# Second gate product by seven products, with its weight sums made in the up stages and half of the late embedding after the last MLP

## The chip, the cores and the metric

The kernel runs on one core of a Trainium2 chip. The metric is the device time of one execution in microseconds (us), and the number to predict is the median over several runs. A core has five engines that each execute their own queue of instructions in order: PE (matrix products), DVE (elementwise vector work), ACT (scalar functions and casts), POOL, and SP, which here issues the DMAs. They meet at semaphores.

## The reference

Two layers on `x` of 1024 tokens by 1024 features in fp32. Layer 0 mixes tokens by a convolution module, layer 1 by sliding-window attention; both then have an MLP of 4096 hidden features and a gated embedding. The part around the change is the end of each layer:

```python
x = layer_norm(DEEPNORM_ALPHA * x + y, mix_ln_g[i], mix_ln_b[i])
x = layer_norm(DEEPNORM_ALPHA * x + sq_relu_mlp(x, mlp_w_up[i], mlp_w_down[i]),
               mlp_ln_g[i], mlp_ln_b[i])
x = x + (p[i] @ ple_w_proj[i]) * jax.nn.sigmoid(x @ ple_w_gate[i])
```

`p[i] @ ple_w_proj[i]` (1024x256 by 256x1024) is called the embedding below, `x @ ple_w_gate[i]` (1024x1024 by 1024x1024) the gate.

## The kernel before

**Precision.** An fp32 operand is split into two fp32r parts: ACT casts the hi part, DVE subtracts it to get the lo part (`split`). Each product is three matmuls, hi·hi, hi·lo and lo·hi (`mm3`, 565), each 128x512 as a rule. So each product of 128 rows, 128 inner and 512 columns costs PE three matmuls, and each operand costs an ACT cast and a DVE subtraction before PE can use it.

**Buffers.** Each tag of `SLOTS` (line 54) is a small set of buffers in SBUF; `wh` and `wl` hold five weight units (128x1024 hi and lo), `ps` and `tr` the PSUM banks, `zz` and `v` one buffer each. `self.x[t]` holds token tile t as two 128x512 halves; `xTh`/`xTl` hold the transposed tokens, hi and lo. `Stream` (484) loads weight units in order as slots come free and splits them: `add` appends, `get` takes, `done` frees, `pump` loads.

**Stages.** `program` (line 1840 on) runs `conv`, `mlp(0)`, `ple(0)`, `attention`, `mlp(1)`, `ple(1)`. `attention` ends with `embed(1, (0, 1), "t")` (1713): 16 groups of 6 matmuls that compute the embedding of layer 1, copied to SBUF and stored to DRAM (`proj`), to be read back by `ple`. `mlp` (1225) works by seven products instead of eight (Strassen-Winograd) in its up half, a loop over pairs of hidden blocks numbered `m`, and in its down half (`down_seven`, 1367), whose last call adds up `x`, lets DVE and POOL do the layer norm of tiles 0 to 7 and transposes each tile by PE into PSUM, from where `to_xT` (603) splits it into `xTh`/`xTl`. Two pairs of each up half (`SUMS`) also make sums of down weights (`down_sums`, 1110). `ple` (1442) is the plain gate product: two column halves of four weight units, per token tile 24 matmuls per half, then sigmoid on ACT, multiply and add on DVE, and the store to `out`. Token tile 7's second half is done in two 256-column pieces (`last_tile`), so that little remains after the last matmul.

**Order.** A list scheduler (`Recorder.schedule`, 341) simulates the engines with a table of costs and fixes the queue of every engine. Instructions are taken by when their inputs are ready, then by a priority, the order of the program plus the shift of a `later(...)` block. All instructions are emitted by one line, L480, hence that line in every row of the profile. Nothing is reordered at run time: an instruction that waits holds all behind it on its engine.

Of the kernel before, what the change touches and what calls it, by code (L numbers as in the profile page):

```python
# [21 lines left out]
HT = 512  # L22
# [38 lines left out]
             ps=6, tr=2, sc=0, pv=0)  # L61


LATE = 100
EMBED_BY = 150
HELD, HELD_BY = 6, 200
HEAD = (4, 2)
# [20 lines left out]
SLACK = 900.0  # L88
LOADED = 1500.0
# [393 lines left out]
class Stream:  # L483


    def __init__(self, em):
        self.em = em
        self.units = []
        self.tiles = []
        self.head = 0  # L490
        self.freed = 0

# [20 lines left out]
class Emit:  # L513
    def __init__(self, tc, d):
        self.tc = tc
        self.nc = Recorder()
        self.d = d
        self.hid_tags = ("A", "X")


    def const(self, name, shape, dt):
# [78 lines left out]
    def blocks(self, a):  # L600
        return [a[:, j * P : (j + 1) * P] for j in range(4)]

    def to_xT(self, xt, t):

        for q in range(2):
            pv = self.transpose4(self.blocks(xt[q]), SLACK).rearrange("p (a b) -> p a b", a=4)
            sl = (slice(None), slice(4 * q, 4 * q + 4), slice(t * P, (t + 1) * P))
            self.split(pv, self.xTh[sl], self.xTl[sl])

    def phases_to_xT(self, h):  # L610

# [20 lines left out]
    def layer_norm(self, t, gb, spill=None):  # L632

        nc = self.nc
        xt = self.x[t]
        mean, scale = self.stats(xt)
        for q in range(2):
            nc.vector.scalar_tensor_tensor(out=xt[q], in0=xt[q], scalar=mean, in1=gb[0][q], op0=ALU.subtract, op1=ALU.mult)
        for q in range(2):
            nc.vector.scalar_tensor_tensor(out=xt[q], in0=xt[q], scalar=scale, in1=gb[1][q], op0=ALU.mult, op1=ALU.add)  # L640
        self.to_xT(xt, t)
# [467 lines left out]
    def down_sums(self, i, k):  # L1109
# [12 lines left out]
            nc.sync.dma_start(self.wsum[i][n][:, cols], out)  # L1122
        nc.slack = 0.0

    def first_operands(self, i):
# [111 lines left out]
    def mlp(self, i):  # L1237
        nc, d, ws = self.nc, self.d, self.ws
        tags, xtags = (dict(zip((2, 1, 3, 4), "XAEB")), "EB") if i == 0 else (dict(zip((2, 1, 3, 4), "XEAB")), "AB")
        first, pairs = list(range(HEAD[i])), list(range(HEAD[i], NFF, 2))  # L1240
        ws.add(*[d["w_up"][i, f] for f in first])
        for f in pairs:
            ws.add(*self.pair_units([d["w_up"][i, f + k] for k in range(2)]))

        us = ws.get(len(first))
        for h in range(2):
            for f in first:
                self.store(i, f, (f % 2, h), self.up(f, h, us[f]))
# [100 lines left out]
    def down_seven(self, i, cs, ready, end):  # L1349

        nc, d = self.nc, self.d
        sub = ALU.subtract
        n = len(cs)

        def A(tag, what):
            return [self.quarter(tag, self.hid[i][c, what]) for c in cs]
# [47 lines left out]
        if ready:  # L1404
            one = product(ready, [(0, 0)])
# [6 lines left out]
            two = product(spot(A("wh", "s3"), S(3), 1, 0), [(1, 1)])  # L1412
# [4 lines left out]
        a11, b11 = A("wh", (0, 0)), B("wl", 0, 0)  # L1417
# [11 lines left out]
        product(formed(s2, t2), [(1, 0)], one)  # L1429
        product(formed(A("wh", "s1"), t1), [(1, 1)], one)  # L1430
        s4 = A("wh", "s4")
        if end:
            gb = self.load_row("g", d["mlp_g"][i : i + 1]), self.load_row("g", d["mlp_b"][i : i + 1])
        product(formed(s4, b22), [(0, 1)], one, last=end)
# [5 lines left out]
    def ple(self, i):  # L1440
        nc, d, ws = self.nc, self.d, self.ws
        for cc in range(2):
            ws.add(*[d["w_gate"][i, cc, u] for u in range(4)])
        for cc in range(2):
            us = ws.get(4)
            cs = slice(cc * HT, (cc + 1) * HT)
            for g in GATE_GROUPS[i][cc]:
                if i == 1 and cc == 1 and NT - 1 in g:
                    self.last_tile(us, cs)
                    break  # L1450
                pss = self.tok_group(g, us)
                for ps, t in zip(pss, g):
                    xt = self.x[t][cc]
                    pr = self.sb("t")
                    nc.sync.dma_start(pr, self.proj[i][t][:, cs])
                    s = self.sb("t")
                    nc.scalar.activation(s, ps, AF.Sigmoid)
                    nc.vector.tensor_tensor(out=s, in0=s, in1=pr, op=ALU.mult)
                    nc.vector.tensor_tensor(out=xt, in0=xt, in1=s, op=ALU.add)
                    if i == 1:  # L1460
                        nc.sync.dma_start(d["out"][t * P : (t + 1) * P, cs], xt)
                    else:
                        h, f = t // PH, t % PH
# [3 lines left out]
            ws.done(4)  # L1467

    def last_tile(self, us, cs):

# [141 lines left out]
    def attention(self):  # L1612
# [189 lines left out]
    def program(self):  # L1802
# [36 lines left out]
        self.wsum = [{k: nc.tile(f"wsum{i}_{k}", (P, 1024), F32, "DRAM") for k in range(1, 5)} for i in range(2)]  # L1839
        self.ws = Stream(self)  # L1840
        self.setup()
        self.conv()
# [116 lines left out]
```

## Time and profile before

| | us |
|---|---|
| median of 3 runs | 2125.28 (2124.98 to 2126.82) |
| the profiled execution | 2127.52 |
| span of its instructions | 2125.8 |
| PE busy in the span | 2115.8 (100%) |
| PE weight loads busy | 1762.0 (83%) |
| DVE busy | 1560.1 (73%) |
| ACT busy | 1046.2 (49%) |
| POOL busy | 201.1 (9%) |

The span is from the first to the last instruction of the slowest (here the only) core; the profiled execution is longer by 1.7 us that lie around it. In rows of a timeline the first number is the start in us from the span's start, the second the duration, then engine, line, operation, `out<-in` with the names of buffers, and the shape; brackets hold idle time before the instruction and what ended it. In rows of windows each engine has its busy time in the window and, in brackets, how many instructions that is.

### The profile page before, as it was taken

The page shows a single profiled execution, that of the slowest core. Times are in us where ns is not written, and L with a number is a line of the kernel's source. Part 1 is how long each engine was busy: PE and PEld are TensorE (multiplying, and loading weights), DVE is VectorE, ACT ScalarE, POOL GpSimd, SP SyncE. Part 2 cuts the span into 40 slices and gives each one's busy share as a digit, 9 for nine tenths or more (in the row PEclk, how much of TensorE's full clock was granted, in tenths as well). Part 3 has the DMA queues.
Part 4 walks back from the last instruction along what each step waited for, and adds up shares of the span by engine and source line. Part 5 has one row for each costly group of instructions (what it writes and reads, how often), then busy time and mean ns, then how long its engine had stood idle before and what let it go on. Part 6 is the DMA issues. An engine that isn't in the chain of part 4 may idle for free.

```text
span 2125.8 us, 28547 instructions
## 1 busy us (share of the span) xinstructions
PE 2115.8 (100%) x10067; PEld 1762.0 (83%) x10067; DVE 1560.1 (73%) x2359; ACT 1046.2 (49%) x1888; POOL 201.1 (9%) x391
## 2 busy tenths in 40 slices
PE   9999999999999999999999999999999999999999
PEld 7888888888888888888889888888888888888887
DVE  8766868966566787889554798796755658878993
ACT  7555743555555433341333797365555563333321
POOL 0000141000000200000000566100000011000010
PEclk9999999999999999999999999999999999999999
DMA  7679882347457955540567672364654598445223
GB/s 249 195 204 278 279 216 99 105 163 258 168 179 277 257 184 172 179 129 25 167 194 224 213 239 63 111 197 146 223 187 136 182 339 238 149 160 189 88 70 104
DMA packets 208078, 384.61 MB, mean 181 GB/s; under 512 B 28736, under 2 KB 82496, under 8 KB 207936
## 3 DMA queue, kind: packets, MB, share of 16 engines
q1 hardware_dynamic: 200880, 369.96, 53.0%
q0 software_dynamic: 6912, 12.59, 3.3%
q8 instruction: 79, 1.29, 0.2%
q14 instruction: 63, 0.52, 0.1%
q10 hardware_dynamic: 144, 0.26, 0.0%
HBM read 263.98 MB, written 114.56 MB: 178 GB/s over the span
## 4 chain that ended last, share of the span: by engine, by line
PE 95%; DVE 2%; DMA 2%; ACT 1%; issue 0%; POOL 0%; SPq 0%; DVEq 0%; ACTq 0%; POOLq 0%
PE ps L480 73%; PE tr L480 22%; DMA raw<-in_w_up_dram 1%; DVE A L480 1%; DVE wl L480 0%; DMA wh<-hid 0%; ACT z L480 0%; DVE sm L480 0%; DMA X<-in_xT_dram 0%; ACT t L480 0%; DVE t L480 0%; ACT wh L480 0%; DVE xTl L480 0%; POOL sm L480 0%; SPq L480 0%
## 5 line engine op out<-in xcount | busy, mean ns | idle before, releaser
L480 DVE TENSOR_TENSOR wl<-raw,wh 128x1024 fp32r<-128x1024 f32 (+2 forms) x144 | 151.6, 1053 | 141.4 <-ACT wh L480 141.1
L480 PE MATMUL ps<-xTl,xTh 128*128 128x512 f32 x628 | 244.3, 389 | 0.0
L480 PE MATMUL ps<-xTh,xTl 128*128 128x512 f32 x628 | 244.3, 389 | 0.0
L480 PE MATMUL ps<-xTh 128*128 128x512 f32 x628 | 244.1, 389 | 0.0
L480 PE MATMUL ps<-xTh,wh 128*128 128x512 f32 x608 | 238.7, 393 | 0.4 <-ACT xTh L480 0.3
L480 PE MATMUL ps<-xTl,wh 128*128 128x512 f32 x608 | 238.6, 392 | 0.1
L480 PE MATMUL ps<-xTh,wl 128*128 128x512 f32 x608 | 237.8, 391 | 0.0
L480 ACT CAST wh<-raw 128x1024 fp32r<-128x1024 f32 (+2 forms) x144 | 131.4, 913 | 200.8 <-PE ps L480 98.4
L480 PE MATMUL ps<-wl,xTh 128*128 128x512 f32 (+1 forms) x424 | 162.3, 383 | 0.0
L480 PE MATMUL ps<-wh,xTh 128*128 128x512 f32 (+1 forms) x424 | 161.5, 384 | 0.0
L480 PE MATMUL ps<-wh,xTl 128*128 128x512 f32 (+1 forms) x424 | 160.8, 380 | 0.4 <-DVE xTl L480 0.4
L480 DVE TENSOR_TENSOR wl<-g,wh 128x512 fp32r<-128x512 f32 x140 | 92.5, 686 | 90.0 <-ACT wh L480 90.0
L480 ACT CAST wh<-g 128x512 fp32r<-128x512 f32 x140 | 82.7, 621 | 150.1 <-PE ps L480 98.3
L480 ACT CAST xTh<-wh 128x1024 fp32r<-128x1024 f32 x78 | 81.9, 1050 | 123.2 <-PE ps L480 101.5
L480 PEld LDWEIGHTS ps<-xTl,xTh 128*128 128x128 f32 x628 | 117.9, 188 | 24.6
L480 PEld LDWEIGHTS ps<-xTh,xTl 128*128 128x128 f32 x628 | 117.9, 188 | 24.4
L480 PEld LDWEIGHTS ps<-xTh 128*128 128x128 f32 x628 | 117.9, 188 | 24.3
L480 PEld LDWEIGHTS ps<-xTh,wh 128*128 128x128 f32 x608 | 114.3, 188 | 25.8 <-ACT xTh L480 1.0
L480 PEld LDWEIGHTS ps<-xTh,wl 128*128 128x128 f32 x608 | 114.2, 188 | 23.4
L480 PEld LDWEIGHTS ps<-xTl,wh 128*128 128x128 f32 x608 | 114.3, 188 | 22.2 <-DVE xTl L480 0.8
L480 DVE TENSOR_TENSOR xTl<-wh,xTh 128x1024 fp32r<-128x1024 f32 x78 | 95.1, 1220 | 32.9 <-ACT xTh L480 32.8
L480 DVE TENSOR_TENSOR xTl<-wl,xTh 128x1024 fp32r<-128x1024 f32 x80 | 97.3, 1218 | 3.4 <-ACT xTh L480 3.4
(318 smaller groups left out, 4952.6 us busy)
## 6 DMA issues: line engine op xcount, KB each, us to landing
wh<-hid SPq DMA_DIRECT2D x80, 512.0 KB, 4.5
raw<-in_w_up_dram SPq DMA_DIRECT2D x64, 512.0 KB, 3.8
wl<-in_w_down_dram SPq DMA_DIRECT2D x60, 512.0 KB, 4.6
hid<-t SPq DMA_DIRECT2D x95, 256.0 KB, 2.4
hid<-zz SPq DMA_DIRECT2D x68, 256.0 KB, 3.5
raw<-hid SPq DMA_DIRECT2D x30, 512.0 KB, 4.3
z<-scr SPq DMA_DIRECT2D x32, 256.0 KB, 3.9
proj<-t SPq DMA_DIRECT2D x32, 256.0 KB, 3.8
```

The costliest lines, as they stand in the source:

```text
L480: getattr(getattr(nc, o.eng), o.name)(*a, **k)
```

## The change

- The gate of layer 1 (`ple_seven` in place of `ple(1)`) is done by seven products of quarters (512 tokens by 512 inner by 512 columns) in place of eight.
- Its sums of weights are made by `gate_sums` at four pairs in all of the two up loops (`GATE_SUMS`). Each call loads four 128x512 pieces of `w_gate`, makes four sums on DVE, splits them (ACT casts to the tag `zz`, DVE subtractions) and stores hi and lo to DRAM (`gpart`). `gate_made` later loads them straight into `wh` and `wl`, two 512 KB loads per unit in place of one load and a split.
- The forms of tokens that the seven products need are made after the last layer norm by `row_forms`. For tiles 0 to 3 ACT also copies each transposed half to a buffer `rows[t]`. For tiles 4 to 7 DVE does eight operations of 128x512 per tile (`s3`, `s2`, four lo parts, `s1`, `s4`) where it did two lo parts; four further lo parts follow in `ple_seven`.
- `attention` ends with the embedding of column half 0 alone (8 groups of 6 matmuls); half 1 is called between `mlp(1)` and `ple_seven`, where the two units of `pT` are loaded and split once more. `AHEAD` gives the stream's loads from there on an earlier priority.
- In the last products, partial sums that PE no longer keeps in PSUM are copied by ACT and added by DVE (`copy`, `plus`): 12 copies and additions. Tile 7 has two 256-column pieces again.

```diff
+AHEAD = 300
+GATE_SUMS = (7, 9), (1, 3)
+GATE_TAG = 'zz'
...
     def pump(self):
...
-            self.tiles.append(u() if callable(u) else self.em.prep(u))
+            with self.em.nc.later(-self.ahead):
+                self.tiles.append(u() if callable(u) else self.em.prep(u))
...
+    def turned_copy(self, to, t, q):
+        pv = self.transpose4(self.blocks(self.x[t][q]), SLACK)
+        self.nc.scalar.copy(to, pv)
+        return to
+
+    def row_forms(self, xt, t):
...
+        if t < 4:
...
+            for q in range(2):
+                self.turned_copy(self.rows[t][q], t, q)
+                hi, lo = self.spot(q, t)
+                v = self.rows[t][q].rearrange("p (a b) -> p a b", a=4)
+                self.split(v, hi, lo)
+            return
+        r = self.rows[t - 4]
+        p0, p1 = (self.transpose4(self.blocks(xt[q]), SLACK) for q in range(2))
...
+        s3 = self.sb("z")
+        tt(out=s3, in0=r[0], in1=p0, op=sub)
+        s2 = self.sb("z")
+        tt(out=s2, in0=p1, in1=s3, op=sub)
+        self.split(four(p1), *self.spot(1, t))
+        x2 = [self.sb("X", F32R) for k in range(2)]
+        self.split(s2, *x2)
+        tt(out=r[0], in0=s2, in1=r[0], op=add)
+        w = self.sb("E", F32R, 2 * HT)
+        x1 = w[:, 0:HT], w[:, HT : 2 * HT]
+        self.split(r[0], *x1)
+        tt(out=r[1], in0=r[1], in1=s2, op=sub)
+        self.split(four(s3), *self.spot(0, t))
...
+    def gate_sums(self, k):
...
+        for j, q, tag in ((0, 0, "v"), (0, 1, "A"), (1, 1, "z"), (1, 0, "z")):
+            b[j, q] = self.sb(tag)
+            cols = slice(k % 2 * HT, (k % 2 + 1) * HT)
+            nc.sync.dma_start(b[j, q], self.d["w_gate"][1, q, 2 * j + k // 2][:, cols])
...
+        for n, out, x, y in ((1, b11, b12, b11), (3, b12, b22, b12), (2, b22, b22, b11), (4, b21, b21, b22)):
+            nc.vector.tensor_tensor(out=out, in0=x, in1=y, op=sub)
+            hs[n] = out
+        for n in (3, 1, 4, 2):
+            hi, lo = self.sb(GATE_TAG, F32R), hs[n].bitcast(F32R)
+            nc.scalar.copy(hi, hs[n])
+            nc.sync.dma_start(self.gpart[n, 0][:, cols], hi.bitcast(F32))
+            nc.vector.tensor_tensor(out=lo, in0=hs[n], in1=hi.bitcast(F32), op=sub)
+            nc.sync.dma_start(self.gpart[n, 1][:, cols], hs[n])
...
+            if m in GATE_SUMS[i]:
+                self.gate_sums(GATE_SUMS[i].index(m) + i * len(GATE_SUMS[0]))
...
+    def ple_seven(self, i):
...
+        order = [[w[0, 0], w[0, 1]], [w[0, 2], w[0, 3]]]
+        made = {n: [lambda n=n, u=u: self.gate_made(n, u) for u in range(2)] for n in range(1, 5)}
+        order += [made[2], made[1], [w[1, 2], w[1, 3]], made[3], made[4]]
...
+        us = ws.get(2)
+        two = [self.ps() for t in range(5)]
+        pieces = [(t, two[t], slice(0, HT)) for t in range(3)]
+        pieces += [(3, two[3 + k][:, 0:256], slice(k * 256, (k + 1) * 256)) for k in range(2)]
+        for t, ps, cols in pieces:
+            part(ps, F[3], us, t, False, cols)
+            finish(t + 4, 1, plus(c22[t][:, cols], ps), cols)
+        ws.done(2)
+        us = ws.get(2)
+        for t, ps, cols in pieces:
+            part(ps, plain[1, 1], us, t, True, cols)
+            finish(t + 4, 0, plus(c21[t][:, cols], ps), cols)
...
-        self.embed(1, (0, 1), "t")
+        self.embed(1, (0,), "t")
...
-        self.ple(1)
+        self.ws.ahead = AHEAD
+        self.embed(1, (1,), "t")
+        self.ple_seven(1)
```

How the queues change at three places:

**DVE in the last layer norms.** `B_...` are halves of a token tile, `sm` its statistics, `g` the gains, `xTl` the lo part of the transposed tokens. Before, where the lo parts of tile 4 stand between the layer norms of tiles 5 and 6:

```order
2287 L480 SCALAR_TENSOR_TENSOR B_2857_16007<-B_2857_16007,sm_3038_18032,g_3001_17652 128x512
2288 L480 SCALAR_TENSOR_TENSOR B_2858_16009<-B_2858_16009,sm_3038_18032,g_3002_17657 128x512
2289 L480 SCALAR_TENSOR_TENSOR B_2857_16007<-B_2857_16007,sm_3040_18050,g_3004_17673 128x512
2290 L480 TENSOR_TENSOR xTl_341<-ps_3056_18196,xTh_340 128x4x128
2291 L480 TENSOR_TENSOR xTl_341<-ps_3058_18234,xTh_340 128x4x128
2292 L480 SCALAR_TENSOR_TENSOR B_2858_16009<-B_2858_16009,sm_3040_18050,g_3005_17678 128x512
2293 L480 BN_STATS sm_3042_18064<-B_2861_16017 128x6
2294 L480 BN_STATS sm_3047_18104<-B_2863_16021 128x6
2295 L480 TENSOR_TENSOR xTl_341<-tr_3059_18238,xTh_340 128x4x128
2296 L480 BN_AGGR sm_3043_18069<-sm_3042_18064 128x2
```

Now the lines of tile 5, where `z` is `s3` and `s2`, `bo` the buffers of `rows[1]`, and `X` and `E` the lo parts of the forms that the products read:

```order
2336 L483 SCALAR_TENSOR_TENSOR B_2885_16067<-B_2885_16067,sm_3076_18143,g_3031_17709 128x512
2337 L483 TENSOR_TENSOR z_2895_16102<-bo_2838_15890,tr_3113_18336 128x512
2338 L483 SCALAR_TENSOR_TENSOR B_2887_16072<-B_2887_16072,sm_3076_18143,g_3032_17714 128x512
2339 L483 TENSOR_TENSOR z_2897_16122<-ps_3128_18410,z_2895_16102 128x512
2340 L483 TENSOR_TENSOR xTl_349<-z_2895_16102,xTh_348 128x4x128
2341 L483 TENSOR_TENSOR bo_2838_15890<-z_2897_16122,bo_2838_15890 128x512
2342 L483 TENSOR_TENSOR xTl_349<-ps_3128_18410,xTh_348 128x4x128
2343 L483 TENSOR_TENSOR X_3082_18164<-z_2897_16122,X_3080_18160 128x512
2344 L483 TENSOR_TENSOR E_3083_18165<-bo_2838_15890,E_3083_18165 128x512
2345 L483 TENSOR_TENSOR bo_2894_16100<-bo_2894_16100,z_2897_16122 128x512
2346 L483 SCALAR_TENSOR_TENSOR B_2885_16067<-B_2885_16067,sm_3084_18167,g_3034_17730 128x512
2347 L483 SCALAR_TENSOR_TENSOR B_2887_16072<-B_2887_16072,sm_3084_18167,g_3035_17735 128x512
```

Two instructions of a tile have become eight, in front of the next tile's layer norm, and the later tiles stand behind them.

**PE at the same place.** The change's rows in which the second sum of weights (`wh_3122`, `wl_3121`, `wh_3132`) meets tiles 5 and 6; `X_3082` is the lo form of tile 5 above, `X_3090` that of tile 6, made at row 2357 of DVE, 14 rows behind `X_3082`:

```order
8658 L483 MATMUL ps_3110_18315<-wh_3132_18461,X_3082_18164 128x512
8659 L483 MATMUL tr_3130_18447<-ident_346,B_2885_16067 128x128 x4
8660 L483 MATMUL tr_3136_18504<-ident_346,B_2887_16072 128x128 x4
8661 L483 MATMUL ps_3114_18346<-wh_3122_18368,X_3089_18222 128x512
8662 L483 MATMUL ps_3114_18346<-wl_3121_18367,X_3089_18222 128x512
8663 L483 MATMUL ps_3114_18346<-wh_3122_18368,X_3090_18224 128x512
8664 L483 MATMUL ps_3114_18346<-wh_3122_18368,X_3089_18222 128x512
8665 L483 MATMUL ps_3114_18346<-wl_3121_18367,X_3089_18222 128x512
```

Before, in the same stage, PE had products of `xTh` and `xTl` alone, and the transposes stood between matmuls of tiles that were done; now the forms of tile 6 are wanted two transposes and 12 matmuls behind the first use of tile 5's.

**The last instructions on DVE.** Before, `t` is the gate and `B` the tile:

```order
2345 L480 TENSOR_TENSOR t_3110_18740<-t_3110_18740,t_3109_18707 128x512
2346 L480 TENSOR_TENSOR B_2861_16017<-B_2861_16017,t_3110_18740 128x512
2347 L480 TENSOR_TENSOR t_3112_18751<-t_3112_18751,t_3111_18746 128x256
2348 L480 TENSOR_TENSOR B_2865_16025<-B_2865_16025,t_3112_18751 128x256
2349 L480 TENSOR_TENSOR t_3112_18751<-t_3112_18751,t_3111_18746 128x256
2350 L480 TENSOR_TENSOR B_2865_16025<-B_2865_16025,t_3112_18751 128x256
```

Now, where `g` holds the partial sum of the gate:

```order
2417 L483 TENSOR_TENSOR g_3145_18598<-g_3145_18598,ps_3178_18829 128x512
2418 L483 TENSOR_TENSOR g_3146_18603<-g_3146_18603,ps_3181_18849 128x256
2419 L483 TENSOR_TENSOR g_3145_18598<-g_3145_18598,t_3191_18957 128x512
2420 L483 TENSOR_TENSOR g_3146_18603<-g_3146_18603,t_3192_18964 128x256
2421 L483 TENSOR_TENSOR B_2885_16067<-B_2885_16067,g_3145_18598 128x512
2422 L483 TENSOR_TENSOR B_2889_16076<-B_2889_16076,g_3146_18603 128x256
2423 L483 TENSOR_TENSOR g_3146_18603<-g_3146_18603,ps_3184_18867 128x256
2424 L483 TENSOR_TENSOR g_3146_18603<-g_3146_18603,t_3193_18984 128x256
2425 L483 TENSOR_TENSOR B_2889_16076<-B_2889_16076,g_3146_18603 128x256
```

Each piece has an addition of the last product (`ps`) ahead of sigmoid, and the chain of the second piece stands behind four rows of tile 6 and of the first piece.

More of the change, by code (lines that the diff above doesn't have):

```diff
@@ L489, in __init__ @@
         self.tiles = []
+        self.ahead = 0
         self.head = 0
@@ L518, in __init__ @@
         self.hid_tags = ("A", "X")
+        self.seven = False
     def const(self, name, shape, dt):
@@ L601, in blocks, with spot @@
         return [a[:, j * P : (j + 1) * P] for j in range(4)]
+    def spot(self, q, t):
+        sl = (slice(None), slice(4 * q, 4 * q + 4), slice(t * P, (t + 1) * P))
+        return self.xTh[sl], self.xTl[sl]
     def to_xT(self, xt, t):
@@ L606, in to_xT, with four @@
             pv = self.transpose4(self.blocks(xt[q]), SLACK).rearrange("p (a b) -> p a b", a=4)
-            sl = (slice(None), slice(4 * q, 4 * q + 4), slice(t * P, (t + 1) * P))
-            self.split(pv, self.xTh[sl], self.xTl[sl])
+            self.split(pv, *self.spot(q, t))
+    def turned_copy(self, to, t, q):
[3 more added lines that the diff above has]
+    def row_forms(self, xt, t):
+        nc = self.nc
+        tt, sub, add = nc.vector.tensor_tensor, ALU.subtract, ALU.add
+        if t < 4:
+            tags = (("zz",), ("bo", "bo"), ("v", "A"), ("t", "t"))[t]
+            if len(tags) == 1:
+                w = nc.tile(tags[0], (P, 1024), F32)
+                self.rows[t] = w[:, 0:HT], w[:, HT : 2 * HT]
+            else:
+                self.rows[t] = [self.sb(x) for x in tags]
+            for q in range(2):
[6 more added lines that the diff above has]
+        p0, p1 = (self.transpose4(self.blocks(xt[q]), SLACK) for q in range(2))
+        def four(v):
+            return v.rearrange("p (a b) -> p a b", a=4)
+        s3 = self.sb("z")
[11 more added lines that the diff above has]
+        self.split(four(s3), *self.spot(0, t))
+        for n, x in ((2, x2), (1, x1)):
+            self.rforms[n][t - 4] = [[v[:, k * P : (k + 1) * P] for v in x] for k in range(4)]
+        for n, at in ((3, t), (4, t - 4)):
+            x = self.spot(0, at)
+            self.rforms[n][t - 4] = [[v[:, k] for v in x] for k in range(4)]
     def phases_to_xT(self, h):
@@ L640, in layer_norm @@
             nc.vector.scalar_tensor_tensor(out=xt[q], in0=xt[q], scalar=scale, in1=gb[1][q], op0=ALU.mult, op1=ALU.add)
+        if self.seven:
+            self.row_forms(xt, t)
+            return
         self.to_xT(xt, t)
@@ L1431, in down_seven @@
         s4 = A("wh", "s4")
+        self.seven = end and i == 1
+        if self.seven:
+            self.rows = [None] * 4
+            self.rforms = {n: [None] * 4 for n in range(1, 5)}
         if end:
@@ L1467, in ple, with part, finish, plus @@
             ws.done(4)
+    def ple_seven(self, i):
+        nc, d, ws = self.nc, self.d, self.ws
+        w = d["w_gate"][i]
+        order = [[w[0, 0], w[0, 1]], [w[0, 2], w[0, 3]]]
+        made = {n: [lambda n=n, u=u: self.gate_made(n, u) for u in range(2)] for n in range(1, 5)}
+        order += [made[2], made[1], [w[1, 2], w[1, 3]], made[3], made[4]]
+        ws.add(*[u for p in order for u in p])
+        plain = {
+            (a, h): [[[x[:, k + 4 * a, t * P : (t + 1) * P] for x in (self.xTh, self.xTl)] for k in range(4)]
+                     for t in range(4 * h, 4 * h + 4)] for a, h in ((0, 0), (1, 0), (1, 1))
+        }
+        F = self.rforms
+        def part(ps, A, us, t, more=False, cols=slice(0, HT)):
+            tr = []
+            for k in range(4):
+                o = k % 2 * HT
+                ws_ = slice(o + cols.start, o + cols.stop)
+                tr.append((*A[t][k], *[x[:, ws_] for x in us[k // 2]]))
+            self.mm3(ps, tr, not more, True, more)
+        def finish(t, q, src, cols=slice(0, HT)):
+            n = cols.stop - cols.start
+            at = slice(q * HT + cols.start, q * HT + cols.stop)
+            pr = self.sb("t")[:, 0:n]
+            nc.sync.dma_start(pr, self.proj[i][t][:, at])
+            s = src if src.buf.space != "PSUM" else self.sb("t")[:, 0:n]
+            nc.scalar.activation(s, src, AF.Sigmoid)
+            nc.vector.tensor_tensor(out=s, in0=s, in1=pr, op=ALU.mult)
+            xt = self.x[t][q][:, cols]
+            nc.vector.tensor_tensor(out=xt, in0=xt, in1=s, op=ALU.add)
+            nc.sync.dma_start(d["out"][t * P : (t + 1) * P, at], xt)
+        def plus(v, ps):
+            nc.vector.tensor_tensor(out=v, in0=v, in1=ps, op=ALU.add)
+            return v
+        def copy(ps, tag):
+            v = self.sb(tag)
+            nc.scalar.copy(v, ps)
+            return v
+        us = ws.get(2)
+        one = [self.ps() for t in range(4)]
+        c11 = []
+        for t in range(4):
+            part(one[t], plain[0, 0], us, t)
+            c11.append(copy(one[t], "t"))
+            self.split(self.rows[t][1].rearrange("p (a b) -> p a b", a=4), *self.spot(0, t))
+        ws.done(2)
+        us = ws.get(2)
+        for t in range(4):
+            ps = self.ps()
+            part(ps, plain[1, 0], us, t)
+            finish(t, 0, plus(c11[t], ps))
+        ws.done(2)
+        us = ws.get(2)
+        c21 = []
+        for t in range(4):
+            part(one[t], F[2], us, t, True)
+            c21.append(copy(one[t], "g"))
+        ws.done(2)
+        us = ws.get(2)
+        c22 = []
+        for t in range(4):
+            part(one[t], F[1], us, t, True)
+            c22.append(copy(one[t], "z"))
+        ws.done(2)
+        us = ws.get(2)
+        for t in range(4):
+            part(one[t], F[4], us, t, True)
+            finish(t, 1, one[t])
+        ws.done(2)
+        us = ws.get(2)
+        two = [self.ps() for t in range(5)]
[4 more added lines that the diff above has]
+            finish(t + 4, 1, plus(c22[t][:, cols], ps), cols)
+        ws.done(2)
+        us = ws.get(2)
+        for t, ps, cols in pieces:
+            part(ps, plain[1, 1], us, t, True, cols)
+            finish(t + 4, 0, plus(c21[t][:, cols], ps), cols)
+        ws.done(2)
@@ L1839, in program @@
         self.wsum = [{k: nc.tile(f"wsum{i}_{k}", (P, 1024), F32, "DRAM") for k in range(1, 5)} for i in range(2)]
+        names = [f"gpart{n}_{k}" for n in range(1, 5) for k in range(2)]
+        for n in names:
+            nc.slots(n, [n])
+        gate = {n: nc.tile(n, (P, 4 * HT), F32, "DRAM") for n in names}
+        self.gpart = {(n, k): gate[f"gpart{n}_{k}"] for n in range(1, 5) for k in range(2)}
         self.ws = Stream(self)
```

14 lines of the change are left out of this document (added).

## The prediction

> **What bounds the kernel now.** I read the page's table of engines first, then the waits of PE, then the end of the chain of waits.
>
> ```profile
> span 2125.8 us, 28547 instructions
> PE 2115.8 (100%) x10067; PEld 1762.0 (83%) x10067; DVE 1560.1 (73%) x2359; ACT 1046.2 (49%) x1888; POOL 201.1 (9%) x391
> ```
> ```profile
> PE ps L480 <- DVE t L480: 1.5, 1, 1.5
> PE ps L480 <- ACT t L480: 1.2, 2, 0.7
> PE ps L480 <- DVE A L480: 0.7, 2, 0.5
> ```
> ```profile
> 2096.81 13.60 PE ps L480 x60
> 2110.41 5.44 PE tr L480 x24
> 2115.85 5.76 PE ps L480 x48
> ```
>
> PE works all but 10 of 2125.8 us; its three largest named waits come to 3.4 us (total, times, longest). The chain's end is matmuls back to back: 13.60/60 = 0.2267 us for one of 128x512, 5.76/48 = 0.12 for one of 128x256. So a matmul less is worth 0.2267 us, wherever PE stays fed. Whether it does is read stage by stage, first in the last products of the MLP (start, length, then busy time and count on PE, its weight loads, DVE, ACT, POOL, then clock and DMA):
>
> ```profile
> 2015.71:2028.40 12.69, 12.69 (x65) 10.57 (x64) 12.69 (x23) 3.40 (x5) 1.48 (x4) 1.00 0.01 2
> 2040.00:2050.00 10.00, 10.00 (x54) 8.32 (x53) 10.00 (x18) 2.35 (x4) 1.69 (x5) 1.00 0.01 2
> 2050.00:2060.00 10.00, 10.00 (x54) 8.39 (x53) 10.00 (x16) 4.38 (x7) 1.99 (x2) 1.00 0.14 54
> 2060.00:2070.00 10.00, 10.00 (x46) 8.24 (x45) 6.71 (x11) 3.44 (x5) 0.00 (x0) 1.00 0.83 252
> ```
>
> Here DVE is as full as PE: 10.00 of 10. PE doesn't wait only because it still has products whose operands exist. This is where the change adds work to DVE.
>
> **The change part by part.** All times are in the clock of the trace before; what comes off ahead of a stage moves it bodily.
>
> *Matmuls.* The order has 8419 matmuls of 128x512 before and 8371 now: 8 products become 7, and 48 go (4 tiles of 12). 48 x 0.2267 = 10.88 us, the gain if PE never waits. From the first matmul of the last two MLP products to the end both orders have 408 of 128x512, 48 of 128x256 and 64 transposes, since 48 of the embedding come in there; the 10.88 us leave where the embedding stood, after attention.
>
> *The forms of the last layer norms.* DVE's rows that I price by, and PE's two anchors:
>
> ```profile
> 1977.38 1.23 DVE L480 TENSOR_TENSOR xTl<-wh,xTh 128x1024 fp32r<-128x1024 f32 x1 [0.36 <-ACT xTh L480]
> 1978.53 0.68 DVE L480 TENSOR_TENSOR B<-B,ps 128x512 f32<-128x512 f32 x1
> 2036.13 1.86 DVE L480 BATCH_NORM_STATS2 sm<-B 128x6 f32<-128x512 f32 x3
> 2037.92 0.66 DVE L480 TENSOR_TENSOR xTl<-ps,xTh 128x512 fp32r<-128x512 f32 x1
> 2039.11 0.19 DVE L480 BATCH_NORM_AGGREGATE sm<-sm 128x2 f32<-128x12 f32 x1
> 2039.22 0.63 DVE L480 BATCH_NORM_STATS2 sm<-B 128x6 f32<-128x512 f32 x1
> 2039.78 2.71 DVE L480 SCALAR_TENSOR_TENSOR B<-B,sm,g 128x512 f32<-128x512 f32 x4
> 2042.42 0.20 DVE L480 BATCH_NORM_AGGREGATE sm<-sm 128x2 f32<-128x12 f32 x1
> 2045.08 1.27 DVE L480 TENSOR_TENSOR xTl<-ps,xTh 128x512 fp32r<-128x512 f32 x2
> 2060.02 0.67 DVE L480 TENSOR_TENSOR xTl<-ps,xTh 128x512 fp32r<-128x512 f32 x1
> 2060.62 0.67 DVE L480 TENSOR_TENSOR A<-A,t 128x512 f32<-128x512 f32 x1
> ```
> ```profile
> 2015.71 3.57 PE L480 MATMUL ps<-E,X 128*128 128x512 f32 x15
> 2019.12 0.60 PE L480 MATMUL ps<-ident,A 128*128 128x128 f32 x4
> 2019.47 0.48 PE L480 MATMUL ps<-E,X 128*128 128x512 f32 x1
> 2019.79 0.38 PE L480 MATMUL tr<-ident,A 128*128 128x128 f32 x2
> ```
>
> From start to start, since durations overlap: 0.60 us for 512 elements of tensor-tensor (2060.02 to 2060.62), 1.15 for 1024 (1977.38 to 1978.53; 1.135 over many), 0.60 for statistics (three in 1.79), 0.115 for an aggregate, 0.66 for scalar-tensor-tensor (four in 2.64). To test them on a long stretch: before, rows 2187 to 2289 of DVE's queue are 14 x 1.135 + 47 x 0.602 + 23 x 0.66 + 13 x 0.60 + 6 x 0.115 = 67.9, so from 1977.38 the lo parts of tile 4 (row 2290) should start at 2045.2; the trace has 2045.08. The sum is good to some 0.2 us.
>
> The same from the same split in the changed queue (row 2218; ahead of it both queues have the same products' work): to `X_3082`, the lo form of tile 5, 18 x 1.135 + 61 x 0.602 + 26 x 0.66 + 15 x 0.60 + 7 x 0.115 = 84.1, done at 2061.5 less 0.3; to `X_3090` of tile 6, 18 x 1.135 + 71 x 0.602 + 28 x 0.66 + 16 x 0.60 + 8 x 0.115 = 92.2, done at 2069.6 less 0.3. PE: four transposes lengthen 2019.12 to 2019.79 by 0.67 - 0.23 = 0.44 to 0.48 with the next pair, 0.12 each. From 2015.71 it has 170 matmuls and 48 transposes to the first use of `X_3082`, 44.3 us, so it is there at 2060.0; 182 and 56 to `X_3090`, 48.0 us, at 2063.7. So PE waits 1.3 us for tile 5 and, 1.3 late, 2069.4 - 2065.0 = 4.4 for tile 6, 5.7 in all. Behind these two the order keeps 3 embedding groups and `X_3093` of tile 7 is in time by 2 us. Adjacent dependent instructions on DVE (`s3` to `s2`) and transposes behind a layer norm cost a little more: I take 6.2. Bounds: 4.9 if DVE enters the stretch 1 us earlier, 8.0 if each dependent pair costs its 0.1 and a bank of PSUM is late besides. ACT, at 2.35 to 4.38 of 10, covers the copies of `rows`; POOL isn't touched.
>
> [...]
>
> *The end.*
>
> ```profile
> 2121.64 0.38 ACT L480 ACTIVATE t<-ps 128x256 f32<-128x256 f32 x1 [2.49 <-PE ps L480]
> 2122.05 0.43 DVE L480 TENSOR_TENSOR t<-t,t 128x256 f32<-128x256 f32 x1 [1.99 <-ACT t L480]
> 2122.51 0.42 DVE L480 TENSOR_TENSOR B<-B,t 128x256 f32<-128x256 f32 x1
> ```
>
> PE ends at 2115.85 + 5.76 = 2121.61; the last addition ends 1.3 us later. Now an addition of 0.36 comes ahead of sigmoid, and on DVE tile 6's rows and the first piece's stand in front of it: working the nine last rows through with 0.60 and 0.36 (tile 6's product ends 2.9 us ahead of PE's end, the first piece's 1.4), `plus` of the last piece starts 1.0 us after PE's end, sigmoid ends at 1.85, the last addition at 2.7. That is +1.4; 0.4 (the addition alone) to 2.0.
>
> *The start of the second MLP.* Half of the embedding, 10.88 us of PE's cover, is taken from here:
>
> ```profile
> 1400.00:1410.00 10.00, 10.00 (x49) 8.23 (x49) 9.97 (x17) 8.16 (x15) 0.00 (x0) 1.00 0.87 306
> 1430.00:1440.00 10.00, 10.00 (x46) 8.29 (x45) 9.96 (x17) 6.76 (x12) 0.00 (x0) 1.00 0.46 131
> 1440.00:1450.00 10.00, 10.00 (x46) 8.29 (x45) 8.56 (x16) 5.69 (x11) 0.00 (x0) 1.00 0.12 34
> ```
>
> DVE is full to about 1440 with the token forms (9.97 of 10). In the new order PE takes the first pair's plain products, then mixes products of forms 2 and 3 as their parts come with 24 plain matmuls of the next pair; by the sum above the parts are there within a microsecond. I take 1.0 us, between 0 and 4.
>
> *Up stages.* Per call of `gate_sums` 8 DVE operations, 4.8 us, 4 casts and 12 DMAs; the DVE and ACT that it loads have room, and the stores of `zz` bound the pace, the one buffer being reused after its store:
>
> ```profile
> 500.00:600.00 100.00, 99.35 (x437) 81.57 (x436) 62.88 (x97) 53.47 (x89) 0.00 (x0) 1.00 0.60 202
> 1500.00:1600.00 100.00, 99.50 (x439) 82.01 (x438) 66.25 (x102) 53.50 (x89) 0.00 (x0) 1.00 0.61 203
> ```
> ```profile
> hid<-zz SPq DMA_DIRECT2D x68, 256.0 KB, 3.5
> ```
>
> 3.5 us to landing make DVE wait some 2.3 us up to three times a call, behind which stand the splits of the next weights and, behind them, PE. With 34 to 37 us free in 100 and calls two pairs apart I take 0.3 us in all four; 0 to 3. If the cover were gone, a call's 4.8 + 6.9 would show.
>
> *Loads at the end.* The made units save 8 splits of 1.135 us on DVE. Two loads of 512 KB stand where one did, and one second unit is wanted 18 matmuls after its slot comes free, about as long as it takes to land; 0.3 us of the 6.2 is for that.
>
> Sum: -10.88 + 6.2 + 1.4 + 1.0 + 0.3 = -1.98 us. The profiled execution has a span of 2125.8 and 2127.52 in all; I expect a span near 2123.8 and lay the same difference on the median: 2125.28 - 1.98 = **2123.3 us**. By the bounds of all terms it goes from -5.6 to +6.1, in the likeliest case from 2120 to 2128.
>
> **The rivals.**
>
> *A. DVE keeps up.* The second half of the embedding stands in this very stage as cover; if DVE comes to the forms 6 us earlier, for instance because it starts the stretch ahead or the transposes come sooner, the tail's term is gone: -10.88 + 1.4 + 1.0 + 0.3 = -8.2, 2117.1. For it: 10.88 us of cover were added against 2 operations of 1024 and 6 of 512 for each tile of 4 to 7. Against it: DVE has no idle time in the three windows, and the forms stand in its queue where they stand.
>
> *B. The start of the second MLP decides.* If PE has nothing else ready there, DVE's forms end when they did, and PE waits for the whole cover taken: +10.88 in place of +1.0, in sum +7.9, 2133.2. It decides from the point where forms are more than the 24 plain matmuls (5.4 us) late. For it: DVE at 9.97 of 10 for 40 us. Against: PE didn't wait anywhere in these windows, so before there was slack, and the order fills with the next pair.
>
> *C. The up stages pay.* If a call's stores and their waits hold the splits of the next pair, PE waits for part of 11.7 us: 1.5 us a call make +6 in place of +0.3, 2129. For it: one buffer `zz`, and each unit that comes late is waited for in turn. Against: a third of DVE is free.
>
> *D. The change doesn't take the matmuls off PE.* Excluded by the order's counts.
>
> **How the numbers follow.** The forecast has 0.58, A 0.17, B 0.14, C 0.09, the rest is unforeseen. Runs of this kernel spread by 1.84 us, so about 0.2%, 4.25 us, can be told from no change: below 2121.0 is faster, above 2129.5 slower. Faster: A and a fifth of the forecast, 0.17 + 0.12 = 0.29. Slower: B, half of C and the unforeseen, 0.20. Same: 0.51. The range takes in A and most of C and leaves out B: 2116 to 2130; the forecast's own is 2120 to 2128.
>
> **What would show it.** Right: two waits of PE on DVE `X`, some 1 and 4 us, near 2050 to 2059 of the new span; DVE at 10 of 10 until about 2070 - 11; the last addition 2.7 us after PE's last matmul; no named wait of PE over 1 us in the up stages. Wrong: no wait on `X` (A), over 5 us of waits on DVE's forms or lo weights between 1385 and 1430 (B), waits on `wl` or `wh` in the up loops (C). The prediction falls, too, if PE's step in the new span isn't 0.2267.

## The result and the profile after

| | before | with the change |
|---|---|---|
| median | 2126.82 us (22 runs, 2124.98 to 2129.0) | 2129.91 us (22 runs, 2127.79 to 2131.9) |
| span of the profiled execution | 2125.8 us | 2128.7 us |

The ratio is 1.0014 (95% interval 1.0007 to 1.002): 3.1 us slower, where 2.0 us faster was forecast. The change in time is inside the 0.2% that the prediction called "same", but its sign is the other one, and the interval leaves out no change. The time itself, 2129.91 us, lies at the upper end of the range of 2116 to 2130 and outside the forecast's own 2120 to 2128. The page's head and the waits of PE in the profile after (engine, what it waited for, total us, times, longest):

```profile
span 2128.7 us, 28707 instructions
PE 2110.5 (99%) x10019; PEld 1753.8 (82%) x10019; DVE 1604.0 (75%) x2435; ACT 1072.8 (50%) x1937; POOL 202.1 (9%) x391
```
```profile
PE ps L483 <- ACT X L483: 3.6, 2, 3.3
PE ps L483 <- ACT bo L483: 1.7, 3, 0.9
PE ps L483 <- DVE t L483: 1.5, 1, 1.5
PE ps L483 <- ACT t L483: 1.0, 2, 0.7
PE ps L483 <- DVE X L483: 0.9, 2, 0.5
PE ps L483 <- DMA wh<-gpart: 0.9, 1, 0.9
```

PE is idle for 18.2 us of its span (2128.7 - 2110.5) where it was for 10.0. The waits for `X`, for ACT's copy `bo` and for the load of `gpart` are new. Yet 8.2 us more idle time and 10.9 us less work would still make the span 2.7 us shorter. The rest is busy time in which PE did less work: matmuls run slower behind each wait (the first step takes 0.33 to 0.34 us in place of 0.2267), and slowest in the tail (0.42; windows: busy time and counts of PE, its loads, DVE, ACT, POOL, then the granted clock):

```profile
2054.00:2058.00 4.00, 3.44 (x18) 2.74 (x18) 4.00 (x8) 0.63 (x1) 0.00 (x0) 1.00 0.02 4
2058.00:2062.00 4.00, 0.73 (x2) 0.30 (x2) 4.00 (x8) 2.34 (x4) 1.06 (x2) 1.00 0.00 0
2062.00:2066.00 4.00, 3.67 (x10) 2.96 (x11) 4.00 (x7) 1.79 (x3) 0.00 (x0) 0.64 0.01 2
2066.00:2070.00 4.00, 4.00 (x22) 3.25 (x21) 2.66 (x5) 2.50 (x3) 0.00 (x0) 0.93 0.00 0
```

DVE works without a gap until 2066, as before; PE now stands still between 2058 and 2061, and its mean clock from 2062 to 2066 is 0.64 of full speed: 10 matmuls where 18 fit. The same place in PE's timeline (start, duration, what, shapes, in brackets the idle time before and what ended it), and two waits around it:

```profile
2023.58 0.50 PE L483 MATMUL ps<-wh,wh 128*128 128x512 f32 x1 [0.67 <-ACT t L483]
...
2054.33 0.73 PE L483 MATMUL ps<-wh,X 128*128 128x512 f32 x2 [0.37 <-DVE X L483]
...
2056.73 1.03 PE L483 MATMUL tr<-ident,B 128*128 128x128 f32 x8
2061.06 0.50 PE L483 MATMUL ps<-wh,X 128*128 128x512 f32 x1 [3.29 <-ACT X L483]
2061.39 0.40 PE L483 MATMUL ps<-wl,X 128*128 128x512 f32 x1
2062.33 0.74 PE L483 MATMUL ps<-wh,X 128*128 128x512 f32 x2 [0.54 <-DVE X L483]
...
2063.13 1.03 PE L483 MATMUL ps<-wh,X 128*128 128x512 f32 x2
2063.96 0.63 PE L483 MATMUL ps<-wl,X 128*128 128x512 f32 x1
2064.39 1.05 PE L483 MATMUL ps<-wh,X 128*128 128x512 f32 x2
...
2083.30 0.50 PE L483 MATMUL ps<-wh,E 128*128 128x512 f32 x1 [0.88 <-DMA wh<-gpart]
```

The two waits that the prediction named are there: 0.37 us for tile 5, and for tile 6 3.29 us for the hi part and 0.54 for the lo part. With the slow first step of 0.33 us behind each they come to 5.0 us. From 2063.13 to 2064.39 three matmuls take 1.26 us, 0.42 each in place of 0.2267. Eight such steps until 2066.5 cost 8 x 0.20 = 1.6 us.

The other loss lies in the second MLP's up loop, at its early pairs, with the two calls of `gate_sums`. DVE, ACT and PE in that order, and what SP issued before (rows of issues are shown without their waits):

```profile
1503.21 0.33 SPq L483 DMA_DIRECT2D A<-in_w_gate_dram  x1
1503.82 0.33 SPq L483 DMA_DIRECT2D raw<-in_w_up_dram  x1
```
```profile
1509.65 0.69 DVE L483 TENSOR_TENSOR g<-raw 128x512 f32<-128x512 f32 x1 [3.33 <-DMA raw<-in_w_up_dram]
```
```profile
1515.86 0.64 ACT L483 ACTIVATE z<-t 128x512 f32<-128x512 f32 x1 [3.17 <-DVE t L483]
...
1518.09 0.57 ACT L483 COPY bo<-ps 128x512 f32<-128x512 f32 x1
```
```profile
1518.72 0.50 PE L483 MATMUL ps<-xTh,wh 128*128 128x512 f32 x1 [0.92 <-ACT bo L483]
```

A load of `w_up` goes out at 1503.82, behind a load of `w_gate`, and is waited for until 1509.65, 5.8 us, where the median from issue to landing of the loads of `w_up` between 1440 and 1545 is 4.4; DVE stands 3.33 us, ACT then 3.17 us for DVE, its copy of a PSUM bank comes at 1518.09, and PE waits for that bank. Three such waits for `bo` and one for `t` cost some 3 us with the slow first step of 0.33 to 0.34 us behind each, where the kernel before lost less than 1 in the same 100 us.

The end went as forecast: PE's last matmul starts at 2123.09 and takes 0.12, and the last addition ends at 2125.96, 2.75 us later (1.3 before):

```profile
2124.18 0.41 DVE L483 TENSOR_TENSOR g<-g,ps 128x256 f32<-128x256 f32 x1
2125.08 0.42 DVE L483 TENSOR_TENSOR g<-g,t 128x256 f32<-128x256 f32 x1 [0.48 <-ACT g L483]
2125.53 0.43 DVE L483 TENSOR_TENSOR B<-B,g 128x256 f32<-128x256 f32 x1
```

### The profile page after: what moved, and what is told of

Its sections match the earlier page's. It is cut to its first block, busy times and chain, and to the rows that moved or that the text cites. A ratio compares the mean times of both kernels' runs of the same rounds, so it can differ in the third digit from the quotient of the medians.

```text
span 2128.7 us, 28707 instructions
## 1 busy us (share of the span) xinstructions
PE 2110.5 (99%) x10019; PEld 1753.8 (82%) x10019; DVE 1604.0 (75%) x2435; ACT 1072.8 (50%) x1937; POOL 202.1 (9%) x391
## 3 DMA queue, kind: packets, MB, share of 16 engines
q8 instruction: 79, 1.29, 0.3%
## 5 line engine op out<-in xcount | busy, mean ns | idle before, releaser
L483 PE MATMUL ps<-xTh,xTl 128*128 128x512 f32 x648 | 252.4, 390 | 0.0
L483 PE MATMUL ps<-xTl,xTh 128*128 128x512 f32 x648 | 252.4, 390 | 0.0
L483 PE MATMUL ps<-xTh 128*128 128x512 f32 x648 | 252.1, 390 | 0.0
L483 PE MATMUL ps<-wl,xTh 128*128 128x512 f32 (+1 forms) x400 | 152.8, 383 | 0.0
L483 PE MATMUL ps<-wh,xTh 128*128 128x512 f32 (+1 forms) x400 | 152.3, 383 | 0.0
L483 PE MATMUL ps<-wh,xTl 128*128 128x512 f32 (+1 forms) x400 | 151.9, 380 | 0.4 <-DVE xTl L483 0.4
```

Source lines behind the costliest of these rows:

```text
L483: getattr(getattr(nc, o.eng), o.name)(*a, **k)
```

## The experiments

Times are medians; the change stands at 2129.91, the kernel before between 2126.5 and 2126.8 in the same sessions. Ratios are against the kernel before.

### e2: the embedding whole again

```diff
-        self.embed(1, (0,), "t")
+        self.embed(1, (0, 1), "t")
...
-        self.embed(1, (1,), "t")
```

> Both column halves of the late embedding stand after attention again, all else as in the change. Theory (DVE's forms bound the tail, and the moved half is cover for them): PE comes to the forms 10.9 us earlier against DVE, which has 2.3 us less to do, so the waits for X grow from 5.0 to some 12 to 14 us; 1.2 us at the start of the second MLP come back: about 2134 to 2138. Rival (the cover is worth nothing there, since PE would have other products, and it is missed at the start of the second MLP): 1 to 2 us faster than the change, about 2128.5.

Measured 2136.48 us, ratio 1.0043 (1.0029 to 1.0056): 6.6 us slower than the change. PE waits for the forms of tile 5 already, and again for tile 6:

```profile
2049.41 0.50 PE L483 MATMUL ps<-wh,X 128*128 128x512 f32 x1 [2.79 <-ACT X L483]
2050.68 1.15 PE L483 MATMUL ps<-wh,X 128*128 128x512 f32 x2 [0.53 <-DVE X L483]
2058.44 0.50 PE L483 MATMUL ps<-wh,X 128*128 128x512 f32 x1 [2.75 <-ACT X L483]
```

So the moved half is cover that this tail needs, and the second MLP's start misses it by far less. The expected waits for `X` were overestimated (two of 3.3 us, 6.6 in all and not 12 to 14); the rest came up in waits for a PSUM bank (ACT `t`, 1.9 us) and for the load of `gpart` (1.7 us).

### e3: dummy products in the wait

```diff
+                if o is self.warm[0]:
+                    p0, x, y = (v.real() for v in self.warm[1:])
+                    for j in range(11):
+                        nc.tensor.matmul(p0, x, y, start=True, stop=True)
...
         tt(out=s2, in0=p1, in1=s3, op=sub)
+        if t == 6:
+            nc.warm = nc.ops[-1], p0, self.xTh[:, 0, 0:P], self.xTh[:, 0, 0:HT]
```

> 11 matmuls whose result is not used are put on PE between the transposes of tile 6 and the first product that waits for its form; nothing else in any queue is altered. They need 2.5 us of the 3.3 us in which PE stood still, and end as the form is ready. Theory (the granted clock falls to a half for 3.4 us because PE stood still, and this costs 1.6 us): the granted clock stays at 1.00 and the time falls by 1.3 to 1.7 us, to about 2128.4. Rival (the half clock has to do with something else there, or it costs nothing because PE would wait anyway): no gain, or up to 0.5 us lost.

Measured 2128.95 us, ratio 1.001 (1.0001 to 1.0019); by the medians 1.0 us faster than the change, but the two intervals overlap. The windows of the tail show the clock:

```profile
2058.00:2062.00 4.00, 3.02 (x18) 2.45 (x17) 4.00 (x8) 1.05 (x2) 1.07 (x2) 1.00 0.01 4
2062.00:2066.00 4.00, 3.61 (x17) 2.65 (x16) 4.00 (x8) 2.07 (x5) 0.00 (x0) 1.00 0.00 0
```

It stays at 1.00 (three or four of the 17 matmuls from 2062 on are dummies). PE's longest wait there is 0.98 us, where it was 3.29 in the change. That the standing PE brought the half clock on is shown by the trace; its price of 1.6 us comes from the trace of the change, and the medians neither show nor contradict it.

### e4: two sums of each tile on POOL

```diff
-        tt(out=r[0], in0=s2, in1=r[0], op=add)
+        nc.gpsimd.tensor_tensor(out=r[0], in0=s2, in1=r[0], op=add)
...
-        tt(out=r[1], in0=r[1], in1=s2, op=sub)
+        nc.gpsimd.tensor_tensor(out=r[1], in0=r[1], in1=s2, op=sub)
```

> The sums s1 and s4 of tiles 4 to 7 are made by POOL, which has little to do there; DVE has two operations less per tile. Theory (DVE's queue sets when X of tile 6 is ready): tile 6's form comes 2.4 us earlier (4 of 0.60), PE's wait of 4.2 us falls to some 2, and as PE stands still less than before the clock stays at 1.00: 2.5 to 4 us gained, about 2126.5. Rival (POOL's work slows DVE down, or the forms that POOL makes late are waited for next): less than 1 us gained, with waits on POOL or on E.

Measured 2131.07 us, ratio 1.0022 (1.0013 to 1.003), by the medians 1.2 us slower than the change, but the two intervals overlap: no gain, where 2.5 to 4 us were expected. POOL's and DVE's timelines beside each other:

```profile
2052.40 1.63 POOL L483 TENSOR_TENSOR bo<-z,bo 128x512 f32<-128x512 f32 x1 [2.29 <-DVE z L483]
2053.98 1.72 POOL L483 TENSOR_TENSOR bo<-bo,z 128x512 f32<-128x512 f32 x1
```
```profile
2052.78 1.78 DVE L483 SCALAR_TENSOR_TENSOR B<-B,sm,g 128x512 f32<-128x512 f32 x1
2054.49 0.68 DVE L483 TENSOR_TENSOR xTl<-ps,xTh 128x512 fp32r<-128x512 f32 x1
2055.09 1.16 DVE L483 TENSOR_TENSOR X<-z,X 128x512 fp32r<-128x512 f32 x1
```

While POOL works, DVE's instructions with two operands in SBUF take 1.78 and 1.16 us in place of 0.73 and 0.68; the one that reads PSUM (`ps`) keeps its 0.68. Two operations of 0.60 were taken off DVE per tile, and 1.05 + 0.48 = 1.5 us put back. The rival held.

### e5: the forms in two steps

```diff
         tt(out=s2, in0=p1, in1=s3, op=sub)
-        self.split(four(p1), *self.spot(1, t))
         x2 = [self.sb("X", F32R) for k in range(2)]
         self.split(s2, *x2)
-        tt(out=r[0], in0=s2, in1=r[0], op=add)
...
+        with nc.later(400):
+            self.split(four(p1), *self.spot(1, t))
+        with nc.later(400):
+            tt(out=r[0], in0=s2, in1=r[0], op=add)
...
```

> In row_forms, tiles 4 to 7 now take s3, s2 and the X parts first; the lo parts of the plain tokens, s1, the E parts and s4 get a later priority (400). No operation is added or removed. Theory (PE waits for X because DVE's queue has five operations of each earlier tile ahead of it that no product wants yet): X of tile 6 no longer waits for some ten operations of 0.60, the 5.0 us of waits for X and the half clock of 1.6 us go, and part comes back as waits for E: 3 to 6 us gained, 2124 to 2127. Rival (DVE's whole sum up to the last form sets the end of the tail, in whatever order): the waits turn up at E or at the plain lo parts, less than 1 us gained.

Measured 2124.69 us, ratio 0.9992 (0.9983 to 1.0001): 5.2 us below the change. In the tail's windows of e5 and of the change:

```profile
2040.00:2070.00 30.00, 30.00 (x145) 24.77 (x144) 29.71 (x50) 16.53 (x27) 1.94 (x5) 1.00 0.40 138
```
```profile
2040.00:2070.00 30.00, 25.79 (x119) 20.38 (x118) 28.66 (x49) 13.76 (x22) 2.54 (x6) 0.94 0.35 122
```

DVE is as full as it was, with the same instructions; PE has no wait, the clock is 1.00. Not DVE's sum set the tail, then, but what stood in its queue ahead of the forms wanted first. The waits for `X` and the half clock, 6.6 us by the trace of the change, went, and no wait came back at `E`.

### e6, e7: the second loop's sums at later pairs, alone and with e5

```diff
-GATE_SUMS = (7, 9), (1, 3)
+GATE_SUMS = (7, 9), (8, 10)
```

> The second MLP's two calls of gate_sums stand at pairs 8 and 10 in place of 1 and 3. Theory (the early pairs' queue of SP and DVE is crowded by what the MLP's start leaves behind, later pairs have room as in the first loop): the waits on ACT bo and t between 1490 and 1560, 2.9 us with what follows, go: about 2127.3. Rival (a call costs PE some 1.2 us wherever it stands in the second loop): the waits turn up near 1650 to 1750, the time stays within 1 us of the change's.

> e5 and e6 together. If the two costs are apart from each other, the gains add: 5 to 8 us below the change, 2122 to 2125, faster than the kernel before by 1 to 4 us. If a loss only moves, it stays above 2125.

e6 measured 2126.8 us, ratio 1.0 (0.9991 to 1.0009): 3.1 us below the change. e7 measured 2120.93 us, ratio 0.9975 (0.9966 to 0.9985): 5.6 us below the kernel before, 9.0 below the change, so the gains add. The stretch of the waits for `bo` in the change, then in e6, and the waits for PE that are left in the last 120 us of e7:

```profile
1500.00:1560.00 60.00, 58.18 (x253) 46.73 (x252) 43.66 (x68) 32.07 (x55) 0.00 (x0) 1.00 0.79 259
```
```profile
1500.00:1560.00 60.00, 60.00 (x266) 49.65 (x265) 38.52 (x59) 33.04 (x55) 0.00 (x0) 1.00 0.62 207
```
```profile
PE ps L483 <- ACT t L483: 0.7, 1, 0.7
```

e6 kept the tail of the change. Its wait of 3.28 us for `X` ended at 2058.49, and there the clock stayed down for about twice as long as in the change:

```profile
2058.00:2062.00 4.00, 3.47 (x7) 2.32 (x8) 4.00 (x7) 2.08 (x4) 0.00 (x0) 0.50 0.00 0
2062.00:2066.00 4.00, 4.00 (x15) 3.10 (x14) 2.75 (x5) 2.33 (x4) 0.00 (x0) 0.71 0.00 2
```

### e8, e9: the sums alone, in the kernel before

```diff
+GATE_SUMS = (7, 9), (1, 3)
...
+            if m in GATE_SUMS[i]:
+                self.gate_sums(GATE_SUMS[i].index(m) + i * len(GATE_SUMS[0]))
```

(e9: `(7, 9), (8, 10)`. The function is that of the change.)

> The kernel before with gate_sums added at the same four pairs as in the change; what they store is not read, the gate stays at eight products. Theory (the calls alone cost PE the waits in the second loop): 2 to 3 us slower than the kernel before, with waits on ACT bo or t near 1500 to 1560. Rival (the calls are hidden, and those waits come from the rest of the change, such as the halved embedding that leaves DVE behind at the start of that MLP): within 0.7 us of the kernel before.

> The kernel before with gate_sums added as in e8, but the second loop's calls at pairs 8 and 10 in place of 1 and 3; what they store is not read. Theory (calls at early pairs of the second loop are what costs, by loads that land late, and e8's 1.6 us were that): within 0.6 us of the kernel before, and 1 us or more below e8. Rival (16 loads and 32 stores more cost the same wherever they stand): 1.6 us slower than before, like e8.

e8 measured 2128.11 us, ratio 1.0006 (0.9997 to 1.0015), e9 2126.21 us, ratio 0.9999 (0.999 to 1.0008). At late pairs the sums show no cost. At early pairs they cost some 1.6 us by the medians, but the interval holds no change too, and the waits of PE in the profiled execution of e8 name none for `bo`. So the early calls alone don't explain the 3 us of the change. The window of its waits, in e8 and then in e2, the two runs that have the early calls and the whole embedding ahead of the second MLP:

```profile
1500.00:1560.00 60.00, 59.95 (x265) 49.29 (x264) 44.93 (x71) 31.70 (x54) 0.00 (x0) 1.00 0.77 254
1500.00:1560.00 60.00, 58.80 (x260) 48.33 (x259) 43.73 (x69) 31.11 (x53) 0.00 (x0) 1.00 0.76 250
```

The kernel before has 266 matmuls there, as e6 has; the change, e3, e4 and e5, where half of the embedding is moved as well, have 250 to 253. By these profiles most of the loss comes where both parts of the change meet: the calls at early pairs and the shorter cover ahead of the loop, which orders the queues otherwise from 1401 us on. Taking either away shortens it, and e6 takes it away in full. The rival of e8's expectation, the halved embedding, thus holds a part of the truth. The queues of e8 and e2 are the same up to the last products of the second MLP, and yet e2 has 5 matmuls less and a wait of 1.2 us for `bo`; that part goes with when loads land, which differs between these two executions: the same instruction of DVE waits 1.29 us for a load of `w_up` in e2 (until 1535.46) and 0.40 in e8 (until 1535.78). How the two parts make the loads late together was not taken apart further and stays open.

### e1: all four calls in the first loop

```diff
-GATE_SUMS = (7, 9), (1, 3)
+GATE_SUMS = (7, 8, 9, 10), ()
```

> All four calls of gate_sums are made in the first MLP's up loop (pairs 7 to 10) and none in the second's. Theory (in the second up loop the calls' loads and stores hold SP's queue, so loads of w_up land late and ACT's copy that PE's bank waits for comes late; in the first loop two calls cost nothing): PE's waits on ACT bo and t between 1490 and 1560, 2.9 us with what follows them, go, and 2 to 2.8 us are gained: about 2127.4. Rival (it is the calls' own work on DVE and ACT, wherever it stands): the same waits turn up near 500 to 640 in the first loop, and the time stays within 1 us of the change's.

Measured 2158.5 us, ratio 1.0149 (1.0135 to 1.0163): 28.6 us slower than the change; neither theory expected this. The second loop's waits did go. But calls at neighbouring pairs up to the loop's end wait for one another's stores through the one buffer `zz` (ACT waits 9.0 us for the stores from it, seven times), and the loads of the down half behind them come late (ACT waits 4.9 us for one of `w_down` into `zz`). PE's waits there, and a window:

```profile
621.55 0.80 PE L483 MATMUL ps<-xTh,wh 128*128 128x512 f32 x1 [2.14 <-ACT bo L483]
622.14 0.63 PE L483 MATMUL ps<-xTl,wh 128*128 128x512 f32 x1
622.57 0.63 PE L483 MATMUL ps<-xTh,wl 128*128 128x512 f32 x1
...
699.77 0.80 PE L483 MATMUL ps<-xTh 128*128 128x512 f32 x1 [18.11 <-ACT xTh L483]
```
```profile
680.00:700.00 20.00, 1.89 (x5) 0.98 (x5) 4.53 (x5) 4.94 (x7) 0.00 (x0) 0.50 0.57 195
```

### e10: e7 with the embedding whole

The edit of e2 on e7.

> e7 with both halves of the late embedding after attention again. Theory (DVE is full through the tail in any order of the forms, so PE needs the cover): PE waits for X, E or lo parts 6 to 9 us in the last 80 us, the 1.4 us of the second MLP's start come back: 2125 to 2129, against e7's 2120.9. Rival (with the forms in two steps DVE is early enough, and the move only costs the 1.4 us at the start): 2119.5.

Measured 2127.86 us, ratio 1.0004 (0.9996 to 1.0013): 6.9 us slower than e7. The cover is needed with the better order too; the seven products gain what they gain only with the embedding's half in the tail.

## Why the prediction was wrong

The terms of its sum, against the profile after (a step between starts less the pace of 0.2267 us, summed over a place):

| term | predicted | measured |
|---|---|---|
| 48 matmuls less | -10.9 | -10.9; the step is unchanged |
| waits for `X` in the tail | 5.7 of the 6.2 | 5.0 |
| half clock behind them | not in the sum | 1.6 |
| second unit of `gpart`; bank held for a copy | the other 0.5 | 1.1 and 0.9 |
| end | 1.4 | 1.4 |
| start of the second MLP | 1.0 | 1.4 |
| up stages | 0.3 | about 2.5 |
| sum | -2.0 | +3.0 |

**What held.** The matmuls, the place and size of the two waits for tiles 5 and 6, DVE's step of 0.60 us in a full queue (the two rows below), the end, and the start of the second MLP: there e6 and e7, without waits for `bo`, lose 1.4 us between 1401 and 1500 where the kernel before loses nothing. Rival A (DVE keeps up) fell, since PE waited; rival B fell, since the start cost an eighth of the cover taken.

The split from which the queue was counted, and the lo form of tile 6, in the profile after: 1970.30 + 92.2 - 0.3 gives 2062.2, and the row ends at 2062.27.

```profile
1970.30 1.23 DVE L483 TENSOR_TENSOR xTl<-wh,xTh 128x1024 fp32r<-128x1024 f32 x1 [0.18 <-ACT xTh L483]
2061.59 0.68 DVE L483 TENSOR_TENSOR X<-z,X 128x512 fp32r<-128x512 f32 x1
```

**What failed.** The largest error is the step "Up stages": "I take 0.3 us in all four; 0 to 3". It looked at the free third of DVE and at the stores of `zz`. What the rows show in its place is a load of `w_up` that goes out behind a load of `w_gate`, lands late (5.8 us, where the median is 4.4) and goes on through DVE and ACT to a PSUM bank, about 2.5 us in place of 0.3. This is rival C by its result, with another chain than the one it named; e6 settles that the early calls are needed for it, as two constants bring back 3.1 us. The sum also took the change part by part, and e8 and e2 show that these calls cost less without the moved embedding, so this term could not be had from the calls alone. That SP's order of loads and stores by itself makes the loads late is argued from the one chain shown, not tested. The second error is a mechanism that the sum of the tail lacked: a wait of PE was priced at its length. The change's wait of 3.29 us also took the clock down, to 0.64 over 4 us, and in e3's trace, without that wait, it reads 1.00; the change's own steps make that 1.6 us more. A further 1.5 us are small waits for a load and a bank in the tail that were mis-sized. The waits for `X` came out 0.7 us shorter than their term, which hides as much of these errors.

**Where the gain went.** Of 10.9 us, 6.6 were turned into waits for forms and their half clock by the order of DVE's queue (e5 brings back 5.2), 2.5 to 3.1 into late loads (e6), 2.0 into the waits for `gpart` and for a bank in the tail, and 1.4 each into the start and the end: together more than was gained.

## What to carry to other kernels

When a change adds work to an engine that is full while the matrix engine is not waiting, count its queue up to each operand that is wanted, row by row; where that count is late, put what is wanted first ahead before giving the change up: e5 moved no work and gained 5.2 us. A call that is hidden on the compute engines still stands in the DMA queue ahead of loads that others wait for (a load of `w_up` behind one of `w_gate` landed after 5.8 us, where the median was 4.4; two constants brought back 3.1 us in e6), so place it where these have slack, and try another place. Price parts of a change together where they meet in one stage. Price a wait of the matrix engine not at its length alone: behind waits of 2.14 us (e1) to 3.29 us (the change) came a stretch at half clock, which cost 1.6 us in the change and more in e6; nothing came behind the second wait of e2, 2.75 us.

## What the runs showed of the hardware

**The clock fell behind four waits of 2.14 to 3.29 us.** In e1 a wait of 2.14 us without anything beside it was followed by matmuls at steps of 0.43 us from 621.55 to 624.7, and in e1's wait of 18.11 us the window reads 0.50. In the change 3.29 us led to 0.64 over 4 us, in e6 3.28 us to 0.50 over 4 us and 0.71 over the next 4. The same length doesn't always do it: in e2 the first wait, 2.79 us, was followed by a window at 0.60 (2050 to 2054, with steps of 0.42 to 0.43 us from 2051.63 on), the second, 2.75 us until 2058.44, by this one:

```profile
2058.00:2062.00 4.00, 3.03 (x12) 2.10 (x12) 4.00 (x7) 1.63 (x3) 0.00 (x0) 1.00 0.02 4
```

A wait of 0.92 us in the change (for ACT `bo`, until 1518.72) left the clock at 1.00 (1518 to 1522), too. The half clock lasted 3.4 us in the change (2063.1 to 2066.5) and 3.2 us in e1 (621.55 to 624.7), and in e6 about double.

**POOL held up DVE.** In the rows of e4, beside POOL's two operations of 1.63 and 1.72 us, DVE's instructions with two operands in SBUF went from 0.73 to 1.78 us and from 0.68 to 1.16, and the one that read PSUM stayed at 0.68. At tile 6, from 2061.11 on, they took 1.76, 1.15 and 0.68 us.
